# Handing on staging buffers after a modelled delay, two reduction units moved, and rotary's half swap by copies, in a hybrid encoder block

## The chip, the cores and the metric

The kernel runs on one core of one Trainium2 chip. The metric is the device time of one execution in microseconds (us). TensorE (PE) multiplies matrices, VectorE (DVE) and ScalarE (ACT) work on elements, GpSimd (POOL) issues accumulating DMAs here, and SyncE (SP) issues nearly all other DMAs.

## The reference, cut to what matters

The block puts 16 learned tokens ahead of 1024 frames (width 1024) and computes, in float32:

```python
h = h + token_mixer(rmsnorm(h, norm_mix_g), ...)      # 4 mLSTM heads + 4 retention heads
h = h + channel_mixer(rmsnorm(h, norm_ffn_g), ...)    # conv-gated MLP
return rmsnorm(h, norm_final_g)[:, N_META:]

# token_mixer: proj = up @ w_in, split into q, k, v, output gate of each head
# mLSTM heads:     qk = silu(causal_dwconv(q and k)); gated chunk scan; head_norm; * sigmoid(o)
# retention heads: rotary(q), rotary(k); decaying chunk scan; head_norm; * silu(g)
def rotary(t, pos):
    t1, t2 = t[..., : d // 2], t[..., d // 2:]
    return concatenate([t1 * cos - t2 * sin, t1 * sin + t2 * cos], axis=-1)
# then mixed @ w_out;  channel_mixer: (silu(causal_dwconv(u @ w_up)) * (u @ w_gate)) @ w_down
```

## The kernel before

**Matmuls.** Each float32 product is made of three reduced-precision ones (lines L675, L676, L677): every operand is split into a high part (`hi_...`, a cast on ACT, L295) and a rest (`lo_...`, a subtraction on DVE, L300). The big products use Strassen-like sums of 512-wide quarters, so weights are also added and subtracted before use (DVE, L373 to L378).

**Heads.** They are worked on in the order 4, 0, 1, 2, 3, 5, 6, 7 (numbers 0 to 3 are mLSTM heads, 4 to 7 retention heads). For each, PE makes q and k (`pq<h>`), for a pair of heads v (`pv<p>`), and the output gate (`po<h>`). From PE's projections ACT and DVE make `qT` and `kT`: four-tap convolutions (L901, L906) and SiLU (L916) for mLSTM heads, rotary (L915 to L932) for retention heads. Then each head's scan runs over 9 chunks: scores `s` (L1260), `kw` on ACT and `pt` on DVE from them, state update `u`, output `n` (L1309, L1311). At three points of a scan (after chunks 3, 6 and 8) the norm is finished on DVE (L1350) and applied on ACT (L1355), the result is transposed on PE (`tr_0`, `tr_1`, `tr_2`, L1364), multiplied into `mx` on DVE (L1372) and stored to DRAM (`mxd`, L1384).

**Who sets the order.** The Python program deals the work out while it records it. PE's work is the main line (`go`); everything else (`side`: rotary, convolutions, gates, scans) is dealt in between by a planner that compares modelled loads of PE, DVE and ACT (`load`, in us). Generators give up control with `yield` and are moved on once for each PE group (`tick`). `drain` empties the side list at once, with the flag `rush` set. Each engine then runs its list in order, and each DMA queue too: an SP row that waits holds back all SP rows behind it.

**Staging buffers.** Four buffers of 128x1024 take raw weights from DRAM in a fixed list of jobs (`job`, `jload`, L223): a job's load is issued when `jfree` has handed on a buffer. Beside the weights of heads (`raw_q2a` and so on), three kinds of reduction units use these buffers: `w_unit` (L429) loads two blocks of `w_out`, adds them on DVE (L437 to L441) and stores four sums (`wsw`, L443); `m_unit` (L401) loads two blocks, scales and adds them for the meta tokens (L414 to L418) and accumulates them into DRAM (`accd`, a DMA of POOL, L424); `first_right` (L469) loads finished mixer rows (`raw_fr`) and stores their parts (`rone`, `diff`). In the kernel before, `jfree` directly follows the stores, so the next load of a buffer stands right behind them on SP and waits there until they have landed.

**After the heads** comes the product with `w_out` (`pwx`, `pwy`; weights `raw_w_0`, `raw_w_2`, L1072, split as `hi_w` on ACT, L575) and then the MLP (`pup`, `pga`, `pd`), from about 750 us to the end.

Of the kernel before, what the change touches and what calls it, by code (L numbers as in the profile page):

```python
# [65 lines left out]
def body(ctx, tc, h_in, vecs, cst, mask_in, rot, w_v0, w_vp, w_g, w_out, w_up, w_gate, w_down, out):  # L66
# [17 lines left out]
    last = {}  # L84
# [130 lines left out]
    def jload():  # L215
        while jfreed and len(jraw) < min(len(jobs), jcap[0]):
            i = len(jraw)
            nm, srcs = jobs[i]
            jslot[i] = jfreed.pop(0)
# [51 lines left out]
    def busy():  # L271
        return not rush[0] and max(load["DVE"], load["Activation"]) - load["PE"] > 0.5

# [127 lines left out]
    def m_unit(h):  # L401
# [3 lines left out]
        def make():  # L405
            assert {k, k + 1} <= posted, k

            def g():
                yield from jwait(*js)
                x0, x1 = (jget(j) for j in js)  # L410
                for j in range(2):
# [7 lines left out]
                    yield  # L419
                for i, x in enumerate((x1, x0)):  # L420
                    if h == 4:
                        nc.sync.dma_start(accd[i], x)
                    else:
                        G.dma_start(accd[i], x, accum_op=ALU.add)  # L424
                jfree(*js)
# [3 lines left out]
    def w_unit(k):  # L429
        js = [job(f"w{k + 8 * i}", w_out[k + 8 * i]) for i in range(2)]  # L430

        def make():
            def g():
# [7 lines left out]
                V.tensor_tensor(v12, v12, v11, ALU.add)  # L441
                for x, st_, o in ((v22, "65", HB), (v21, "73", HB), (v11, "65", 0), (v12, "73", 0)):
                    nc.sync.dma_start(sums["w", st_, k][:, o:o + HB], x)  # L443
                jfree(*js)
# [24 lines left out]
    def first_right(k):  # L469
        i = job(f"fr{k}", mxd[k])  # L470

        def make():
            assert k in posted, k
            hi, lo = half_tiles(f"fr{k}")

            def g():
# [5 lines left out]
                V.tensor_tensor(a[:, HB:], a[:, :HB], a[:, HB:], ALU.subtract)  # L482
                nc.sync.dma_start(rone[k][:, :HB], hi.bitcast(F32))
                nc.sync.dma_start(rone[k][:, HB:], lo.bitcast(F32))
                nc.sync.dma_start(diff[k], a[:, HB:])
                jfree(i)
# [49 lines left out]
    for f in w_units(3):  # L536
        f()
    u_fm("o", 4, *v_units(0, 0))
    prev = 4
    for p, (a, b) in enumerate(PAIRS):  # L540
# [4 lines left out]
        u_fm("o", b, *(v_units(p + 1, 0) if p < 2 else r_units(2, 3)), *m_units(a))  # L545
# [93 lines left out]
    def first_norm(r):  # L639
# [13 lines left out]
        for i, x in enumerate(xs):  # L653
# [3 lines left out]
            last.setdefault("first", m)  # L657
# [123 lines left out]
    def sig_tasks(h):  # L781
        def f(b):
            AC.activation(sigt[:, b], sigt[:, b], AF.Sigmoid if h < H else AF.Silu)
            done.add(("sig", h, b))
# [104 lines left out]
    def qk_tasks(h):  # L889
# [29 lines left out]
        def rotary(i, r):  # L919
# [5 lines left out]
            V.tensor_tensor(t[0:64, a:b], x[64:128, a:b], A2[64:128, a:b], ALU.mult)  # L925
# [3 lines left out]
            V.tensor_tensor(d[:, a:b], d[:, a:b], t[:, a:b], ALU.add)  # L929
# [400 lines left out]
    def post_steps(h, p):  # L1330
# [28 lines left out]
        def half(b):  # L1359
# [23 lines left out]
            e = min(t1, MB + HB)  # L1383
            nc.sync.dma_start(mxd[i][:, a0 - MA:e - MA], mx[:, :e - a0])  # L1384
# [836 lines left out]
```

## Time and profile before

| | |
|---|---|
| median of 3 runs | 1546.06 us (1544.81 to 1550.42) |
| the profiled execution's own time | 1552.62 us |
| its span, first to last instruction | 1550.5 us |
| PE busy | 1494.9 us (96%) |
| DVE busy | 1109.5 us (72%) |
| ACT busy | 761.8 us (49%) |
| mean granted TensorE clock | 0.983 |

The profile is of one execution. "Busy" is the time in which an engine executes; a wait is put down to the instruction that released it. `L12` is line 12 of the kernel before; names stand as output<-inputs. `PEq`, `SPq` are the issuing sides of an engine.

### The profile page before, as it was taken

Reading aid. Unit: us, or ns where it says so; the run is one execution under the profiler, and the core shown is the slowest. Engines: PE = TensorE matmul, PEld = TensorE weight load, DVE = VectorE, ACT = ScalarE, POOL = GpSimd, SP = SyncE. Lnnn points to the kernel's source line nnn. Section 1 sums busy time; section 2 is a strip of 40 time slices with the busy share of each in tenths; the row PEclk is TensorE's granted clock in tenths of the full one; section 3 lists DMA queues with packets and bytes.
Section 4 is the critical chain, followed back from the end, with each engine's and each line's share of the span. In section 5 each row is a group of like instructions: output and inputs, shape, how many; then the busy total and the mean of one; then the engine's idle time right before and its main releaser. Section 6 shows DMA issues by size and latency. Waiting matters only on the chain.

```text
span 1550.5 us, 25359 instructions
## 1 busy us (share of the span) xinstructions
PE 1494.9 (96%) x9819; PEld 1357.0 (88%) x9819; DVE 1109.5 (72%) x2156; ACT 761.8 (49%) x1459; POOL 85.1 (5%) x144
## 2 busy tenths in 40 slices
PE   6979999998999989989999999999999999999997
PEld 5979999997999988987888998999999999888887
DVE  8886778765877667755787688766666666778656
ACT  5445666745663545454354455444444444434443
POOL 1000000000000000000000001222220000000000
PEclk9989999999999999999999999999999999999998
DMA  7331265325542356498532327887773223933213
GB/s 264 128 110 56 69 203 160 92 77 169 183 112 83 100 190 187 143 306 319 171 125 100 103 85 227 207 215 197 185 190 88 82 82 131 383 104 115 95 42 109
DMA packets 107176, 232.17 MB, mean 150 GB/s; under 512 B 10808, under 2 KB 34048, under 8 KB 106880
## 3 DMA queue, kind: packets, MB, share of 16 engines
q1 hardware_dynamic: 96736, 201.12, 38.9%
q0 software_dynamic: 10176, 29.37, 9.8%
q8 instruction: 77, 1.26, 0.3%
q14 instruction: 43, 0.35, 0.1%
q10 hardware_dynamic: 144, 0.07, 0.0%
HBM read 179.10 MB, written 74.49 MB: 164 GB/s over the span
## 4 chain that ended last, share of the span: by engine, by line
PE 81%; DMA 9%; DVE 7%; ACT 1%; issue 1%; SPq 0%; DVEq 0%; ACTq 0%
PE pdx L675 3%; PE pdx L677 3%; PE pdx L676 3%; PE pup_x L676 2%; PE pup_x L677 2%; PE pup_x L675 2%; PE pga_x L676 2%; PE pga_x L677 2%; PE pga_x L675 2%; PE pdy L675 2%; PE pdy L677 2%; PE pdy L676 2%; PE pwx L676 2%; PE pwx L675 2%; PE pwx L677 2%; DMA accd<-raw_m 2%
## 5 line engine op out<-in xcount | busy, mean ns | idle before, releaser
L575 ACT CAST hi_up<-raw_up 128x512 fp32r<-128x512 f32 (+1 forms) x52 | 36.4, 719 | 107.2 <-PE pga_z L676 60.3
L576 DVE TENSOR_TENSOR lo_ga<-fraw_ga,hi_ga 128x512 fp32r<-128x512 f32 (+1 forms) x52 | 41.9, 808 | 37.7 <-ACT hi_ga L575 37.5
L675 PE MATMUL pup_x<-uh_g,hi_up 128*128 128x256 f32 (+1 forms) x240 | 67.5, 284 | 1.2 <-ACT uh_g L1625 1.2
L676 PE MATMUL pup_x<-ul_g,hi_up 128*128 128x256 f32 (+1 forms) x240 | 67.5, 283 | 0.1
L576 DVE TENSOR_TENSOR lo_up<-raw_up,hi_up 128x512 fp32r<-128x512 f32 (+1 forms) x52 | 41.2, 809 | 35.9 <-ACT hi_up L575 35.1
L677 PE MATMUL pup_x<-uh_g,lo_up 128*128 128x256 f32 (+1 forms) x240 | 66.6, 283 | 0.0
L576 DVE TENSOR_TENSOR lo_d<-rd,hi_d 128x1024 fp32r<-128x1024 f32 (+1 forms) x34 | 37.7, 1113 | 32.9 <-ACT hi_d L575 32.7
L575 ACT CAST hi_ga<-fraw_ga 128x512 fp32r<-128x512 f32 (+1 forms) x52 | 36.4, 718 | 45.8 <-PE pup_z L676 22.9
L677 PE MATMUL pdx<-uh_d,lo_d 128*128 128x512 f32 (+1 forms) x156 | 57.9, 374 | 0.0
L676 PE MATMUL pdx<-ul_d,hi_d 128*128 128x512 f32 (+1 forms) x156 | 57.6, 373 | 0.0
L575 ACT CAST hi_d<-rd 128x1024 fp32r<-128x1024 f32 (+1 forms) x34 | 32.4, 962 | 49.4 <-PE pdy L676 32.6
L677 PE MATMUL pdy<-uh_d,lo_d 128*128 128x512 f32 x132 | 51.7, 392 | 0.0
L676 PE MATMUL pdy<-ul_d,hi_d 128*128 128x512 f32 x132 | 51.3, 389 | 0.0
L675 PE MATMUL pdx<-uh_d,hi_d 128*128 128x512 f32 (+1 forms) x156 | 49.0, 375 | 0.0
L675 PE MATMUL pdy<-uh_d,hi_d 128*128 128x512 f32 x132 | 48.5, 393 | 0.0
L675 PEld LDWEIGHTS pup_x<-uh_g,hi_up 128*128 128x128 f32 x240 | 45.8, 191 | 2.3 <-ACT uh_g L1625 1.4
L676 PE MATMUL pga_x<-ul_g,hi_ga 128*128 128x512 f32 x120 | 47.6, 397 | 0.0
L677 PE MATMUL pga_x<-uh_g,lo_ga 128*128 128x512 f32 x120 | 47.3, 394 | 0.0
L675 PE MATMUL pga_x<-uh_g,hi_ga 128*128 128x512 f32 x120 | 47.3, 394 | 0.0
L676 PEld LDWEIGHTS pup_x<-ul_g,hi_up 128*128 128x128 f32 x240 | 45.8, 191 | 1.1 <-DVE ul_g L1626 0.3
L677 PEld LDWEIGHTS pup_x<-uh_g,lo_up 128*128 128x128 f32 x240 | 44.9, 190 | 0.8
L1260 PE MATMUL s<-qT,kT 128*128 128x128 f32 (+1 forms) x144 | 27.9, 275 | 11.7 <-DVE kT L929 8.7
(1685 smaller groups left out, 5814.9 us busy)
## 6 DMA issues: line engine op xcount, KB each, us to landing
raw_up<-w_up_d SPq DMA_DIRECT2D x22, 512.0 KB, 4.1
fraw_ga<-w_gate_d SPq DMA_DIRECT2D x22, 512.0 KB, 4.3
acts<-cv SPq DMA_DIRECT2D x44, 256.0 KB, 3.4
wsd<-w_down_d POOLq DMA_DIRECT2D x44, 256.0 KB, 6.4
rd<-wsd SPq DMA_DIRECT2D x22, 512.0 KB, 3.4
raw_w<-w_out_d SPq DMA_DIRECT2D x20, 512.0 KB, 5.8
wsw<-raw_w SPq DMA_DIRECT2D x32, 256.0 KB, 2.0
raw_m<-w_out_d SPq DMA_DIRECT2D x14, 512.0 KB, 3.9
```

Of the source, the lines that this page charges most:

```text
L575: AC.copy(hi[:, o:o + n], x)
L576: V.tensor_tensor(lo[:, o:o + n], x, hi[:, o:o + n].bitcast(F32), ALU.subtract)
L675: m.append(PE.matmul(pt, ah, xh_, start=first and k == 0, stop=False, skip_group_check=True))
L676: PE.matmul(pt, ah, xl_, start=False, stop=False, skip_group_check=True)
L677: m.append(PE.matmul(pt, al, xh_, start=False, stop=last and k == n - 1, skip_group_check=True))
L1260: PE.matmul(s[:, :L], k, q, start=True, stop=True)
```

## The change

1. A generator `lag(us)` is added. It gives up control until the planner's modelled PE load has grown by so many us; outside the planned part and under `rush` it returns at once. It stands ahead of the stores of `w_unit`, `first_right`, of the `mx` rows and ahead of the sigmoids and table loads, and, with 8, 5 and 3 us, between a unit's stores and the `jfree` of its buffers.
2. `m_unit` and the `raw_fr` loads wait in the planner for the rows they need, in place of an assertion.
3. Of three `w_unit`s ahead of all heads, one stays; two move behind the output gates of heads 1 and 3.
4. Rotary's two half-width DVE products become two half-width ACT copies (which swap the halves) and one full-width DVE product; the host table has its signs exchanged.
5. For head 4, the gate tasks are dealt between the first and the second half of rotary, and the planner starts with 4 us on DVE and 2 us on ACT.
6. The eight residual loads are written later in the program (`t == 4`). In the first norm, the mark `last["first"]`, behind which the first weight casts are placed, is set at a later copy.

```diff
+    def lag(us):
+        t = load["PE"]
+        while dealt[0] and not rush[0] and load["PE"] - t < us:
+            yield
...
     def jload():
         while jfreed and len(jraw) < min(len(jobs), jcap[0]):
             i = len(jraw)
             nm, srcs = jobs[i]
+            if nm[:2] == "fr" and int(nm[2:]) not in posted:
+                break
...
     def m_unit(h):
...
-            assert {k, k + 1} <= posted, k
-
             def g():
+                while not {k, k + 1} <= posted:
+                    yield
                 yield from jwait(*js)
...
+                yield
                 for i, x in enumerate((x1, x0)):
                     if h == 4:
                         nc.sync.dma_start(accd[i], x)
                     else:
                         G.dma_start(accd[i], x, accum_op=ALU.add)
+                yield from lag(8)
                 jfree(*js)
...
     def w_unit(k):
...
+                yield from lag(1.5)
                 for x, st_, o in ((v22, "65", HB), (v21, "73", HB), (v11, "65", 0), (v12, "73", 0)):
                     nc.sync.dma_start(sums["w", st_, k][:, o:o + HB], x)
+                yield from lag(5)
                 jfree(*js)
...
     def first_right(k):
...
+                yield from lag(1.5)
                 nc.sync.dma_start(rone[k][:, :HB], hi.bitcast(F32))
                 nc.sync.dma_start(rone[k][:, HB:], lo.bitcast(F32))
                 nc.sync.dma_start(diff[k], a[:, HB:])
+                yield from lag(3)
                 jfree(i)
...
-    for f in w_units(3):
+    for f in w_units(1):
         f()
...
-        u_fm("o", b, *(v_units(p + 1, 0) if p < 2 else r_units(2, 3)), *m_units(a))
+        u_fm("o", b, *(v_units(p + 1, 0) if p < 2 else r_units(2, 3)), *m_units(a), *w_units(p < 2))
...
-            last.setdefault("first", m)
+            if r == 0:
+                last["first"] = m
...
     def sig_tasks(h):
         def f(b):
+            yield from lag(1.5)
             AC.activation(sigt[:, b], sigt[:, b], AF.Sigmoid if h < H else AF.Silu)
...
-            V.tensor_tensor(t[0:64, a:b], x[64:128, a:b], A2[64:128, a:b], ALU.mult)
-            V.tensor_tensor(t[64:128, a:b], x[0:64, a:b], A2[0:64, a:b], ALU.mult)
+            AC.copy(t[0:64, a:b], x[64:128, a:b])
+            AC.copy(t[64:128, a:b], x[0:64, a:b])
             yield
             V.tensor_tensor(d[:, a:b], x[:, a:b], A1[:, a:b], ALU.mult)
+            V.tensor_tensor(t[:, a:b], t[:, a:b], A2[:, a:b], ALU.mult)
             V.tensor_tensor(d[:, a:b], d[:, a:b], t[:, a:b], ALU.add)
...
             mix_into(mx[:, :w], a0, t1)
             e = min(t1, MB + HB)
+            if e < t1:
+                V.tensor_copy(mm[:, i], mx[:, e - a0:w])
+            yield from lag(1.5)
             nc.sync.dma_start(mxd[i][:, a0 - MA:e - MA], mx[:, :e - a0])
...
-    side += qk_tasks(4) + gate_tasks + scan[:12]
+    side += qk_tasks(4)[:2] + gate_tasks + qk_tasks(4)[2:] + scan[:12]
...
-        return [(lambda: tables_load(h), 0, lambda: "gates" in done)]
+        def f():
+            yield from lag(3)
+            tables_load(h)
+        return [(f, 0, lambda: "gates" in done)]
     reset()
+    load.update({"DVE": 4.0, "Activation": 2.0})
     go(o_steps(4))
...
-        if t == 1:
+        if t == 4:
             for kb in range(0, KB, 2):
                 for a, b, o in ((0, SB, 0), (SB, T, 16)):
                     nc.sync.dma_start(RT[kb // 2][:, :, a:b], h_in[:, kb:kb + 2, a + o:b + o])
```

How the planner then deals the work is read from the order of each engine's instructions in the two built programs. Lines of the changed kernel stand some 2 to 18 higher (L690 there is L677 before, L1275 is L1260, L1379 is L1364, L920 is L906, L453 is L443, L225 is L223).

**The start of head 4's scan, on PE.** Before, the first score matmul `s_0` stands right behind the first group of head 0's projection `pq0x`:

```order
L675 MATMUL pq0x_1324<-u11h,hi_o_6_0_996 128x264
L676 MATMUL pq0x_1324<-u11l,hi_o_6_0_996 128x264
L677 MATMUL pq0x_1324<-u11h,lo_o_6_0_997 128x264
L1260 MATMUL s_0_1036<-qT_935,kT_936 128x16
L1265 MATMUL s_0_1036<-cs,kT_936 128x128
L675 MATMUL pq0x_1298<-uS2h,hi_q_1_0_1143 128x264
```

Of the change, on PE, `s_0` stands inside the second group of v (`pv0y`), behind all of head 0's q and k:

```order
L690 MATMUL pv0y_1705<-hi_vp_1_0_1551,u12l 128x256
L688 MATMUL pv0y_1705<-hi_vp_1_0_1551,u12h 128x256
L689 MATMUL pv0y_1705<-lo_vp_1_0_1552,u12h 128x256
L1275 MATMUL s_0_1126<-qT_925,kT_926 128x16
L1280 MATMUL s_0_1126<-cs,kT_926 128x128
L690 MATMUL pv0y_1705<-hi_vp_1_0_1551,u12l 128x256
```

It is the PE's row 481 before and row 659 of the change, so 178 rows later.

**The end of head 4's scan.** Before, on DVE, the norm factor `mv_1` (L1350), for which the transposes `tr_1` wait, stands ahead of the last chunk's `pt_8`:

```order
L1349 RECIPROCAL z_1_1534<-z_1_1534 128x3
L1350 TENSOR_SCALAR mv_1_1361<-mv_1_1361,z_1_1534 128x3
L1320 TENSOR_SCALAR C_7_1537<-C_6_1487,u_7_1529 128x256
L1284 TENSOR_SCALAR pt_8_1511<-s_8_1509,cs 128x128
L906 TENSOR_SCALAR kT_1904<-rawk,vec,kT_1904 128x527
L906 TENSOR_SCALAR kT_1904<-rawk,vec,kT_1904 128x512
```

Of the change, on DVE, `pt_8` stands eleven rows ahead of `mv_1` (L1365 there); between them are the splits and sums of head 0's gate weights (three rows ahead of these: `lo_o` twice and one L920, as well) and the convolution taps of head 0's `kT`:

```order
L381 TENSOR_TENSOR raw_o0a<-raw_o0a,raw_o0b 128x512
L920 TENSOR_SCALAR kT_1884<-rawk,vec,kT_1884 128x512
L1364 RECIPROCAL z_1_1540<-z_1_1540 128x3
L1341 BN_STATS bn_7_1546<-v4hi 128x6
L920 TENSOR_SCALAR kT_1884<-rawk,vec,kT_1884 128x526
L384 TENSOR_TENSOR raw_o0a<-raw_o0a 128x512
L920 TENSOR_SCALAR kT_1884<-rawk,vec,kT_1884 128x512
L1341 BN_STATS bn_8_1574<-v4hi 128x6
L1365 TENSOR_SCALAR mv_1_1372<-mv_1_1372,z_1_1540 128x3
```

Behind `mv_1` DVE has two small rows, four L920, one small row and two more L920, and only then `mx_1_0` (L1387 there). Before, on PE, some fifty matmuls of `pv0y` and `pv0x` stand among `s_8`, `n_8`, `tr_1_0` and `tr_1_1`. Of the change, on PE, nothing stands among them:

```order
L1275 MATMUL s_8_1517<-qT_925,kT_926 128x128
L1324 MATMUL n_7_1537<-v4hi,pt_7_1473 128x256
L1326 MATMUL n_7_1537<-C_6_1499,qT_925 128x256
L1324 MATMUL n_8_1567<-v4hi,pt_8_1519 128x256
L1326 MATMUL n_8_1567<-C_7_1543,qT_925 128x256
L1379 MATMUL tr_1_0_1641<-cs,v4lo 128x128
L1379 MATMUL tr_1_0_1641<-cs,v4hi 128x128 x2
L1379 MATMUL tr_1_1_1666<-cs,v4lo 128x128
L1379 MATMUL tr_1_1_1666<-cs,v4hi 128x128 x2
L688 MATMUL pv0y_1705<-hi_vp_5_0_1908,uS4h 128x256
```

What moved is the PE work: the scan now ends at a `drain`, where none is left to stand beside it.

**The loads of head 2's q and k, on SP.** `raw_q2a` is the first weight block of `pq2x`. Before:

```order
L223 DMA raw_m_2965<-w_out_d 128x1024
L1384 DMA mxd_88<-mx_2_1_2772 128x254
L223 DMA raw_m_3009<-w_out_d 128x1024
L223 DMA raw_q2a<-w_g_d 128x1024
L223 DMA raw_q2b<-w_g_d 128x512 x2
L223 DMA raw_vp_11_3127<-w_vp_d 128x1024
```

Of the change, on SP, a moved `w_unit` stands ahead of it, and the buffer that `raw_q2a` takes is that of its second and third stores:

```order
L225 DMA raw_m_2936<-w_out_d 128x1024
L225 DMA raw_m_2969<-w_out_d 128x1024
L225 DMA raw_w_2975<-w_out_d 128x1024
L225 DMA raw_w_3014<-w_out_d 128x1024
L453 DMA wsw_3_151<-raw_w_3014 128x512
L453 DMA wsw_3_159<-raw_w_2975 128x512
L453 DMA wsw_3_151<-raw_w_2975 128x512
L453 DMA wsw_3_159<-raw_w_3014 128x512
L225 DMA raw_q2a<-w_g_d 128x1024
L225 DMA raw_vp_11_3205<-w_vp_d 128x1024
L225 DMA raw_vp_21_3207<-w_vp_d 128x1024
L225 DMA raw_q2b<-w_g_d 128x512 x2
```

Two loads and four stores came ahead of `raw_q2a`; `raw_q2b` now stands behind two loads that take the buffers of the accumulates. `raw_q5a` shows the same change.

More of the change, by code (lines that the diff above doesn't have):

```diff
@@ L472, in make @@
         def make():
-            assert k in posted, k
             hi, lo = half_tiles(f"fr{k}")
@@ L1383, in half @@
             e = min(t1, MB + HB)
+            if e < t1:
+                V.tensor_copy(mm[:, i], mx[:, e - a0:w])
+            yield from lag(1.5)
             nc.sync.dma_start(mxd[i][:, a0 - MA:e - MA], mx[:, :e - a0])
             if e < t1:
-                V.tensor_copy(mm[:, i], mx[:, e - a0:w])
                 posted.add(i)
@@ L2172, in _lay @@
     c, s = np.cos(ang), np.sin(ang)
-    a["rot"] = np.stack([np.concatenate([c, c], 0), np.concatenate([s, -s], 0)], 1).astype(np.float32)
+    a["rot"] = np.stack([np.concatenate([c, c], 0), np.concatenate([-s, s], 0)], 1).astype(np.float32)
     w = f("w_in")[0].reshape(2, 4, P, -1)
```

## The prediction

> **What bounds the kernel now.** I read the page's busy times first, then the table of stretches, then PE's waits, longest first.
>
> ```profile
> PE 1494.9 (96%) x9819; PEld 1357.0 (88%) x9819; DVE 1109.5 (72%) x2156; ACT 761.8 (49%) x1459; POOL 85.1 (5%) x144
> ```
>
> PE is busy for 96% of the span, so the change can win or lose time only where PE stands idle or runs at a lower clock. Columns below: stretch, length, busy time of PE, PEld, DVE, ACT, POOL, granted clock, DMA share, GB/s.
>
> ```profile
> 50.00:75.00 25.00, 25.00 (x212) 25.00 (x211) 24.16 (x36) 9.85 (x16) 0.00 (x0) 1.00 0.26 86
> 98.00:120.00 22.00, 13.27 (x85) 12.00 (x84) 18.26 (x38) 8.22 (x17) 0.00 (x0) 0.77 0.15 48
> 225.00:245.00 20.00, 18.81 (x146) 17.63 (x145) 16.32 (x37) 16.83 (x34) 0.29 (x2) 1.00 0.62 202
> 375.00:400.00 25.00, 19.55 (x136) 18.02 (x135) 16.20 (x41) 15.58 (x32) 1.25 (x3) 0.93 0.84 261
> 530.00:565.00 35.00, 31.04 (x213) 29.46 (x212) 21.97 (x50) 18.53 (x35) 1.72 (x2) 0.90 0.57 172
> 600.00:660.00 60.00, 55.90 (x410) 52.83 (x410) 43.32 (x101) 27.06 (x62) 0.86 (x1) 1.00 0.54 159
> 680.00:700.00 20.00, 16.29 (x98) 15.01 (x96) 7.01 (x22) 10.92 (x23) 0.00 (x0) 0.83 1.04 366
> 950.00:1540.00 590.00, 589.99 (x3446) 521.03 (x3445) 409.94 (x643) 261.56 (x460) 54.05 (x77) 1.00 0.52 151
> ```
>
> From 950 us on PE has no idle time at all: the MLP is out of the question. The idle time lies in the heads: 8.7 us in the second row, 5.5 in the fourth, 4.0 in the fifth, 4.1 in the sixth, 3.7 in the seventh. PE's waits name the releasers (total, times, longest):
>
> ```profile
> PE s L1260 <- DVE kT L929: 8.7, 1, 8.7
> PE pq3x L675 <- ACT hi_o L295: 4.0, 1, 4.0
> PE n L1309 <- ACT n L1322: 3.7, 1, 3.7
> PE pq6x L675 <- ACT hi_o L295: 2.7, 1, 2.7
> PE pq6x L677 <- DVE lo_o L300: 1.2, 1, 1.2
> ```
>
> A stall costs more than its idle time, because the clock falls behind it:
>
> ```profile
> 104.80:115.00 10.20, 4.33 (x20) 4.33 (x21) 8.95 (x19) 1.42 (x4) 0.00 (x0) 0.50 0.32 104
> 388.10:391.50 3.40, 3.30 (x15) 3.30 (x16) 2.54 (x7) 3.34 (x6) 0.00 (x0) 0.50 0.66 251
> 551.90:558.80 6.90, 5.97 (x27) 5.98 (x28) 5.23 (x12) 6.04 (x11) 0.00 (x0) 0.51 0.20 74
> 688.50:695.30 6.80, 5.15 (x20) 4.78 (x21) 3.48 (x9) 5.67 (x9) 0.00 (x0) 0.50 1.04 387
> ```
>
> PE busy at half clock loses half of that time. So head 4's first score costs 8.7 + 2.2 = 10.9 us, head 3's q (`pq3x`) 4.0 + 1.65 = 5.65, head 6's q 2.7 + 1.2 + 3.0 = 6.9, and `n` 3.7 + 2.6 = 6.3.
>
> **The change part by part.** Sums are made against the profiled execution, 1552.6 us (span 1550.5); the median of the runs shown is 6.6 lower, and I carry the difference over to it. Half a per cent, about what a measurement can tell from no change, is 7.7 us.
>
> *Head 4's first score.* DVE has no gap before it: it is the DVE queue that is late with `kT`.
>
> ```profile
> L925 DVE TENSOR_TENSOR kT<-rawq,A x8: 686/695/704, 98.0 to 640.7; 64x528 f32<-64x528 f32 x4, 64x512 f32<-64x512 f32 x4
> ...
> L374 DVE TENSOR_TENSOR raw_o0a<-raw_o0a,raw_o0b 128x512 f32<-128x512 f32 x1 | 0.7, 680 | 0.0
> ...
> L295 ACT CAST hi_vp<-raw_vp 128x512 fp32r<-128x512 f32 x12 | 6.8, 620 | 3.3 <-PE pv0y L677 1.4 <-PE pq0x L676 1.0 <-ACT gsm L1002 0.9
> ```
>
> Two half-width products of 0.695 become one of full width, which I take at the same price: 0.7 less in each of 4 places, 2.8 us of DVE per head. The two units moved away take eight sums of L374's shape (0.68, so 5.4) off DVE as well. And `s_0` stands 178 PE rows later, some 20 us at the 25.00/212 = 0.12 us of the 50 to 75 stretch. 8.2 + 20 us is far over 8.7, so the stall goes: **-10.9** (bounds -10.9 and -8). The 32 ACT copies are not in the trace; the nearest row is the cast of 0.62, so 20 us on an ACT that is half idle, at nothing; at DVE's 0.7 they take 22. Where ACT is late, at most one pair (1.4) is added to a head.
>
> *The end of head 4's scan.* The order shows no PE work between `s_8` and `tr_1_1` but six matmuls and transposes, and on DVE between `pt_8` and `mv_1` two `lo_o`, four taps, L374, L377 and two statistics; then six taps and `mx_1_0`.
>
> ```profile
> L300 DVE TENSOR_TENSOR lo_o<-raw_o0a,hi_o 128x512 fp32r<-128x512 f32 x5 | 3.3, 685 | 0.7 <-ACT hi_o L295 0.7
> L906 DVE SCALAR_TENSOR_TENSOR kT<-rawk,vec,kT 128x512 f32<-128x512 f32 x6 | 4.5, 745 | 0.1
> L1326 DVE BATCH_NORM_STATS2 bn<-v4hi 128x6 f32<-128x256 f32 x4 | 1.7, 424 | 0.7 <-ACT v4hi L1322 0.7
> L1372 DVE SCALAR_TENSOR_TENSOR mx<-tr,vec,sig 128x384 f32<-128x384 f32 x4 | 2.4, 612 | 0.0
> L1355 ACT ACTIVATE v4hi<-v4hi,mv,z 128x256 f32<-128x256 f32 x4 | 2.2, 590 | 0.0
> ```
>
> To `mv_1`: 2 x 0.685 + 2 x 0.68 + 4 x 0.745 + 2 x 0.424 = 6.6, and 0.6 for L1355; PE has about 1.4 of its own work there: 5.8 idle. From `mv_1` to `mx_1_0`, for which `tr_1_1` waits: 6 x 0.745 + 0.6 and small rows, 5.5, less 0.7 of transposes: 4.8. Behind it `pv0y` waits for ACT, which has two table loads and four passes in that time, about 0.7 more. With the 2.2 of clock that followed the 8.7 us stall: **+13.5** (bounds +8, if half of the taps have run earlier, and +17). These rows follow from the order of one queue, so I hold this term for the surest.
>
> *The loads behind moved units.* `raw_q2a` and `raw_q5a` now wait for a unit's third store.
>
> ```profile
> wsw<-raw_w SPq DMA_DIRECT2D x32, 256.0 KB, 2.0
> ...
> wsw<-raw_w SPq DMA_DIRECT2D x4, 256.0 KB, 6.5
> accd<-raw_m POOLq DMA_DIRECT2D x2, 512.0 KB, 8.1
> ...
> raw_q6a<-w_g_d SPq DMA_DIRECT2D x1, 512.0 KB, 5.0
> ```
>
> The first row is the page's, the others are those of 533 to 551 us, where a unit's stores met the accumulates of `accd`: 6.5 in place of 2.0. Such a store and the load behind it take 11.5 us; this is how head 3's and head 6's q came to stall before. In the change heads 2 and 5 have the same rows in the same order (stores, accumulates between them, load). I price each at head 3's 5.65: **+11.3** for both (bounds 0, if the store takes 2.0, and 2 x 6.9). Queued behind `raw_q2a` on SP stand `raw_vp_11`, `raw_vp_21`, which wait for accumulates, and `raw_q2b`, which is used some 6 us of PE work later: covered. The Trainium skill, page "DMA: Bandwidth & Descriptors", section "Queues, rings and completion order", says that each DMA engine serves its queue rows in turn, packet by packet: a store beside one accumulate would then take about 4, an estimate from the 2.0, and both terms together fall to some 6. The row of 6.5 speaks against it.
>
> *Head 1's q.* Its cast now stands on ACT behind head 0's last norm, a table load, a sigmoid and two passes of L1355, and later behind the eight L883.
>
> ```profile
> L783 ACT ACTIVATE sig<-sig 128x1026 f32<-128x1026 f32 x2 | 2.1, 1056 | 0.0
> L916 ACT ACT_TABLE_LOAD x3 | 3.8, 1283 | 1.1 <-DVE qT L906 1.1
> L883 ACT ACTIVATE A<-A,cols 128x128 f32<-128x128 f32 x16 | 5.0, 392 | 3.2 <-DVE A L877 3.2
> ```
>
> 1.28 + 1.06 + 1.2 + 0.6 = 4.1 and a norm of about 2 ahead, beside 2 us of PE work: 4 idle; 1 more for the second load and the L883. With head 3's clock loss, and less the 1.2 us that 225 to 245 shows idle now: **+5.5** (bounds 0 and +9).
>
> *Head 6's q.* The accumulates now stand behind all four stores, and `raw_fr` behind the load: of 6.9 I take **-4.5** (bounds -6.9 and 0).
>
> *`n` at 686.* What is late is not ACT itself:
>
> ```profile
> 688.78 1.04 ACT L575 CAST hi_w<-raw_w 128x1024 fp32r<-128x1024 f32 x1 [7.49 <-DMA raw_w<-w_out_d]
> L1072 SPq DMA_DIRECT2D raw_w<-w_out_d x1: 383/383/383, 673.9 to 673.9; - x1
> ```
>
> ACT waited 7.5 us in its queue for `raw_w_2`, issued at 673.9 behind eight `wone` loads, and the copy of `n` stood behind. In the change that load directly follows `raw_w_0` and the cast stands behind two more copies of `n`: **-6.3** (bounds -6.3 and 0). Next late is that cast's product, `pwx`, not before the scan's end.
>
> *The rest.* 600 to 660 us holds head 7's rotary, and 4.1 idle; 2.8 less on DVE give back **-2** (bounds -4 and +1.4). Head 3's own rows stay as they were. The later sigmoids, table loads and `mx` stores are waited for by no PE row above; the residual loads move by a few rows on SP; the first norm's mark by one cast: nothing, 2 us either way.
>
> Sum: -10.9 + 13.5 + 11.3 + 5.5 - 4.5 - 6.3 - 2 = +6.6, so 1559.2 in a profile like this one and **1553** as a median.
>
> **The rivals.** *The loads land in time* (faster). If the third store leaves before the accumulates fill the engines, it takes 2.0; `raw_q2a` and `raw_q5a` then come ahead of need, and head 1 loses 1.5. This decides below some 2.6 us of store time. -11.3 - 4: the sum is -8.7, **1537**. For it: the page's median of 2.0; against it: the 6.5. *Half shares*, by the queue rule above: a store of 4.0 leaves about 1.5 idle per head, so the sum falls by 2 x 2.5 to +1.6, **1548**. *The late loads are worse* (slower): heads 2 and 5 at head 6's 6.9 (+2.5), head 1 at 9 (+3.5) and `n` still held by a `raw_w` (+6.3), since 680 to 700 shows the DMA engines at 1.04: +19, **1565**. It decides if the casts of head 1's q find `raw_q1b` not landed. *The change does not do what it says*: excluded for the handing on, since the order shows loads behind the delays; but in a `drain` the delay is nothing.
>
> **How the numbers follow.** Forecast 0.45 (own range 1546 to 1560), in time 0.20, half shares 0.08, worse 0.27. Half of the forecast's chance lies above 1553.8. Faster by over 0.5%: most of "in time" and little else, 0.17. Slower: 0.22 of the forecast and 0.26 of the worse case, 0.48. Within: 0.35. The range reaches from "in time" to a little over "worse": 1537 to 1567.
>
> **What would show it.** The list of PE's waits after: `s` on `kT` gone; `tr` on `z` or `mv` (about 6) and on `mx` (about 4) near 160 us; `pq2x`, `pq5x` on `hi_o` at about 4; `pq1x` on ACT; `n` on ACT gone. I am wrong if the scan's end shows below 6 us, or if `pq2x` and `pq5x` do not wait.

## The result, and the profile after

The changed kernel takes 1560.88 us (median of 7 runs, 1553.46 to 1567.7), the kernel before 1548.18 us in 7 runs of the same sessions: a ratio of 1.0085, 95% interval 1.0057 to 1.0113. It is slower by 0.85%. The profiled execution took 1560.88 us (span 1559.1, mean granted clock 0.981), so 8.3 us more than the profiled execution before. One of the 12 executions of experiment 2 below took 2086.91 us, at a granted clock of 0.654; its ratio leaves it out.

The page's busy times after:

```profile
PE 1496.5 (96%) x9819; PEld 1360.9 (87%) x9819; DVE 1099.6 (71%) x2140; ACT 778.2 (50%) x1488; POOL 84.1 (5%) x144
```

DVE has 10 us less to do and ACT 16 more; the 32 copies alone take 20.0 us on ACT (0.626 each), as forecast. PE is again busy 96% of the time; busy times do not show where 8 us went. The table of stretches does (same columns as in the prediction; L675 of before is L688 here, L1364 is L1379, L1372 is L1387):

```profile
98.00:120.00 22.00, 22.00 (x179) 21.43 (x179) 18.58 (x48) 12.26 (x23) 0.10 (x1) 1.00 0.15 49
150.00:190.00 40.00, 31.59 (x197) 27.43 (x196) 26.97 (x67) 22.12 (x43) 0.43 (x3) 0.83 0.13 41
215.00:250.00 35.00, 29.98 (x208) 28.53 (x207) 21.64 (x55) 21.09 (x42) 0.47 (x3) 0.85 0.69 224
250.00:290.00 40.00, 37.18 (x288) 34.74 (x287) 29.71 (x64) 20.11 (x41) 2.50 (x6) 0.96 0.62 186
440.00:470.00 30.00, 27.23 (x199) 25.18 (x198) 21.03 (x52) 14.05 (x29) 2.55 (x6) 1.00 0.57 159
565.00:600.00 35.00, 28.42 (x217) 27.67 (x216) 21.27 (x39) 15.63 (x29) 0.00 (x0) 0.90 0.66 214
600.00:660.00 60.00, 57.77 (x434) 54.93 (x433) 47.79 (x112) 39.56 (x85) 1.72 (x2) 1.00 0.55 163
680.00:700.00 20.00, 20.00 (x150) 18.58 (x149) 11.70 (x28) 9.94 (x25) 1.72 (x2) 1.00 0.89 267
```

The first and the last row are the two places that were to be cured: 8.7 and 3.7 us of idle time are gone, at full clock. The five rows from 150 to 600 us are the price: 8.4 us idle at the end of head 4's scan, then 5.0, 2.8, 2.8 and 6.6 ahead of the q of heads 1, 2, 5 and 6. The list of PE's waits (total, times, longest) names them:

```profile
PE pq6x L688 <- DVE sig L758: 6.0, 1, 6.0
PE pq3x L688 <- ACT hi_o L302: 4.6, 1, 4.6
PE pq1x L688 <- ACT hi_o L302: 3.9, 1, 3.9
PE tr L1379 <- ACT v4lo L1370: 3.8, 1, 3.8
PE tr L1379 <- DVE mx L1387: 3.2, 2, 2.6
PE pq2x L688 <- ACT hi_o L302: 2.8, 1, 2.8
PE pq5x L688 <- ACT hi_o L302: 2.8, 1, 2.8
```

`s` on `kT` and the long `n` on ACT have left the list. The rows in their place are those that the prediction named, but for `pq3x`, which waited before too, and `pq6x`, which was to get better.

What each place is worth is read, as in the prediction, from the time that PE loses there: its idle time, and half of its busy time at a granted clock of 0.5. PE's work without these losses is nearly the same in both profiles (1476.6 and 1476.2 us), so the losses hold the whole difference but for 0.4 us. Both profiles are read over the same stretches; the changed kernel comes to the same work up to 20 us later, and the edges lie where PE loses nothing in either.

| place | predicted, us | lost before | lost after | change |
|---|---|---|---|---|
| head 4's first score (98 to 120 us) | -10.9 | 10.9 | 0.0 | -10.9 |
| end of head 4's scan (150 to 190) | +13.5 | 0.0 | 12.1 | +12.1 |
| head 1's q (215 to 250) | +5.5 | 1.2 | 8.8 | +7.6 |
| head 2's q (250 to 290) | +5.65 | 0.0 | 4.4 | +4.4 |
| head 5's q (440 to 470) | +5.65 | 0.0 | 2.8 | +2.8 |
| head 6's q (530 to 600) | -4.5 | 7.0 | 8.4 | +1.4 |
| head 7's rotary (600 to 680) | -2 | 4.8 | 2.2 | -2.6 |
| `n` at 686 us (680 to 700) | -6.3 | 6.3 | 0.0 | -6.3 |
| 830 to 850 us | 0 | 0.0 | 3.4 | +3.4 |
| all else (parts of about 3 us at most, of both signs) | 0 | 43.7 | 40.8 | -2.9 |
| **sum** | **+6.6** | **74.0** | **82.9** | **+9.0** |

### The profile page after: what moved, and what is told of

The parts are those of the page before. It is cut to its first block, busy times and chain, and to the rows that moved or that the text cites. A ratio compares the mean times of both kernels' runs of the same rounds, so it can differ in the third digit from the quotient of the medians.

```text
span 1559.1 us, 25372 instructions
## 1 busy us (share of the span) xinstructions
PE 1496.5 (96%) x9819; PEld 1360.9 (87%) x9819; DVE 1099.6 (71%) x2140; ACT 778.2 (50%) x1488; POOL 84.1 (5%) x144
## 4 chain that ended last, share of the span: by engine, by line
PE 79%; DMA 12%; DVE 7%; ACT 1%; issue 1%; SPq 0%; DVEq 0%; POOL 0%; ACTq 0%
PE pdx L688 3%; PE pdx L690 3%; PE pdx L689 3%; PE pup_x L689 2%; PE pup_x L690 2%; PE pga_x L689 2%; PE pup_x L688 2%; PE pga_x L688 2%; PE pga_x L690 2%; PE pdy L688 2%; PE pdy L690 2%; PE pdy L689 2%; PE pv L726 2%; PE pwy L689 1%; PE pwy L690 1%; DMA accd<-raw_m 1%
## 5 line engine op out<-in xcount | busy, mean ns | idle before, releaser
L688 PE MATMUL pup_x<-uh_g,hi_up 128*128 128x256 f32 (+1 forms) x240 | 67.1, 282 | 1.2 <-ACT uh_g L1646 1.2
L690 PE MATMUL pup_x<-uh_g,lo_up 128*128 128x256 f32 (+1 forms) x240 | 66.4, 283 | 0.0
L690 PE MATMUL pdx<-uh_d,lo_d 128*128 128x512 f32 (+1 forms) x156 | 58.0, 375 | 0.0
L690 PE MATMUL pdy<-uh_d,lo_d 128*128 128x512 f32 x132 | 51.8, 392 | 0.0
L688 PE MATMUL pdx<-uh_d,hi_d 128*128 128x512 f32 (+1 forms) x156 | 49.0, 376 | 0.0
L688 PE MATMUL pdy<-uh_d,hi_d 128*128 128x512 f32 x132 | 48.6, 394 | 0.0
L688 PEld LDWEIGHTS pup_x<-uh_g,hi_up 128*128 128x128 f32 x240 | 45.4, 189 | 2.2 <-ACT uh_g L1646 1.4
L690 PE MATMUL pga_x<-uh_g,lo_ga 128*128 128x512 f32 x120 | 47.3, 395 | 0.0
L688 PE MATMUL pga_x<-uh_g,hi_ga 128*128 128x512 f32 x120 | 47.3, 395 | 0.0
L690 PEld LDWEIGHTS pup_x<-uh_g,lo_up 128*128 128x128 f32 x240 | 44.6, 188 | 0.8
L690 PEld LDWEIGHTS pdx<-uh_d,lo_d 128*128 128x128 f32 x156 | 29.3, 188 | 5.6
```

What stands on the lines that cost most here:

```text
L688: m.append(PE.matmul(pt, ah, xh_, start=first and k == 0, stop=False, skip_group_check=True))
L690: m.append(PE.matmul(pt, al, xh_, start=False, stop=last and k == n - 1, skip_group_check=True))
```

## The experiments

Theory A says that the order costs the time: the units that were moved stand ahead of the loads of q, and the side work of head 4 piles up on DVE at the end of its scan. Theory B says that the delays do: everything that is queued later comes later. Times are medians, ratios are to the kernel before, run on the same chip. What one version wins on another goes by their ratios, since the kernel before itself had medians from 1545.33 to 1548.18 us.

**1. No delays.**

```diff
-        while dealt[0] and not rush[0] and load["PE"] - t < us:
-            yield
+        yield from ()
```

> The changed kernel with all its delays at nothing (lag returns at once), all else kept. Theory A, the order: the stall at the end of head 4's scan comes from the DVE queue that the units, the rotary and the gates leave there, and the waits of pq2x and pq5x from the w units that now stand ahead of their loads. Neither needs a delay: near 160 us tr waits about 4 and 2.6 us again (13 us lost there in all), pq2x and pq5x wait about 3 us each, and the time is that of the changed kernel within 4 us. Theory B, the delays: stores, table loads and buffers that come later are what costs; without them the stall at the scan's end and the two waits are gone, and the time falls by 8 us or more, to that of before. Head 6's q: by A its load is as late as in the changed kernel (6 us of wait); by B it waits 3 us or less.

1566.33 us, ratio 1.0123 (1.0100 to 1.0145): the slowest of all, 0.4% above the changed kernel, though the two intervals just overlap (that one ends at 1.0113). Of its waits of PE:

```profile
PE pq5x L687 <- ACT hi_o L301: 4.5, 1, 4.5
PE tr L1378 <- ACT v4lo L1369: 3.8, 1, 3.8
PE n L1323 <- ACT n L1336: 3.3, 1, 3.3
PE pq2x L687 <- ACT hi_o L301: 0.9, 1, 0.9
```

The stall at the scan's end is there to the tenth (3.8), so Theory B falls for it. But A missed half of the rest: without delays `pq2x` waits 0.9 and `pq6x` is not in the list, `pq5x` waits more, and `n` is back. The delays move the waits of q from head to head: at head 6 Theory B had it right (below), at heads 2 and 5 and at `n` neither had. On the whole the delays seem to help; they are not the main cost.

**2. Without the planner's lead at head 4.**

```diff
-    load.update({"DVE": 4.0, "Activation": 2.0})
```

> The changed kernel without the one line that starts the planner of head 4's steps with 4.0 us of DVE and 2.0 us of ACT work on its account, so that it spreads the side work earlier. Theory A, the order: with it the DVE queue at the scan's end is short, since the two weight halves and taps stand elsewhere: near 160 us the tr rows wait no more than 1 us and only n (about 1.2) and pv0y (about 2) wait; 9 us are won there, head 1's q wins 1 to 4 more, pq2x and pq5x wait as in the changed kernel (about 3 us each). The time falls by 8 to 12 us, to about that of before. Rival, the rotary's copies or the moved units alone hold the scan's end: nothing changes there, the time stays within 3 us of the changed kernel.

1551.82 us, ratio 1.0020 (1.0006 to 1.0033): 10 us won with one line. The same stretch as above, in this kernel's table:

```profile
150.00:190.00 40.00, 37.78 (x282) 34.84 (x282) 27.23 (x62) 23.65 (x45) 0.39 (x3) 1.00 0.16 54
```

2.2 us idle in place of 8.4, at full clock: PE loses 2.2 at the scan's end in place of 12.1. So, with all else as changed, the line that accounts 4 us to DVE before head 4 lets the sums, the taps and the splits pile up where PE has nothing else to do. Around head 1's q 7.5 us are lost (190 to 250 us) in place of 8.8, the low end of the 1 to 4 that were to be won; PE there no longer waits for the load, but for DVE (`s` on `pt` 2.1, `tr` on `mx` 1.6).

**3. The old rotary in the changed kernel.**

```diff
-            AC.copy(t[0:64, a:b], x[64:128, a:b])
-            AC.copy(t[64:128, a:b], x[0:64, a:b])
+            V.tensor_tensor(t[0:64, a:b], x[64:128, a:b], A2[64:128, a:b], ALU.mult)
+            V.tensor_tensor(t[64:128, a:b], x[0:64, a:b], A2[0:64, a:b], ALU.mult)
             yield
             V.tensor_tensor(d[:, a:b], x[:, a:b], A1[:, a:b], ALU.mult)
-            V.tensor_tensor(t[:, a:b], t[:, a:b], A2[:, a:b], ALU.mult)
...
-    a["rot"] = ... np.concatenate([-s, s], 0) ...
+    a["rot"] = ... np.concatenate([s, -s], 0) ...
```

> The changed kernel with the rotary of before (two half-width products on DVE, no copies on ACT, the table's sign as before), all else kept. DVE has 2.8 us more per head, ACT 32 copies less. Theory A, the order at one place counts: head 4's first scores wait about 3 us (pq0x), the scan's end loses about 3 in place of 13 because the planner deals the weight halves differently, head 1's q loses 3 to 6: the time falls by 4 to 8 us. Rival, the rotary only moves 22 us from DVE to ACT, and PE waits at the same places: the scan's end still loses 13 and the time is within 3 us of the changed kernel, or above it by up to the 2.8 us of DVE at head 7.

1553.18 us, ratio 1.0037 (1.0018 to 1.0055): 7 us less, with DVE 2.8 us more loaded in each of four heads. The scan's end loses 1.8 (12.1 in the changed kernel), 5.1 are lost around head 4's first scores, from 85 to 120 us (none), and 7.3 at head 1's q (8.8), where 3 to 6 were expected. As A had it, what counts is not the 2.8 us of DVE: the rotary changes what the planner deals where, and so what stands at the scan's end.

**4. The two moved units back at the start.**

```diff
-    for f in w_units(1):
+    for f in w_units(3):
...
-*m_units(a), *w_units(p < 2))
+*m_units(a))
```

> The changed kernel with its two moved w units back ahead of the heads (three at the start, none beside heads 2 and 5), all else kept. Theory A: pq2x and pq5x no longer wait (7 us won with their clock), the scan's end loses about 5 (pv0y on ACT) in place of 13 and head 1's q 2 in place of 7; but the 5.4 us of DVE work return ahead of head 4's first score, where about 7 us are lost (3 at the gate transposes, 4 at pq0x) and 2 of clock: in all 8 to 12 us less than the changed kernel. Rival, the loads are late by the accumulates alone, whatever stands ahead of them: pq2x and pq5x still wait 2 us or more each, and the gain is 5 us or less.

1550.02 us, ratio 1.0009 (0.9991 to 1.0026): 12 us won, and no longer to be told from the kernel before. Its list of PE's waits has no row of `pq2x` or `pq5x`, and in their place:

```profile
PE pv0y L688 <- ACT v L756: 4.3, 1, 4.3
PE n L1324 <- ACT n L1337: 3.8, 1, 3.8
PE pq0x L688 <- ACT rawq L754: 3.4, 1, 3.4
```

**5. The moved units alone, in the kernel before.**

```diff
-    for f in w_units(3):
+    for f in w_units(1):
...
-*m_units(a))
+*m_units(a), *w_units(p < 2))
```

> The kernel before with one part of the change alone: the two w units moved behind the output gates of heads 1 and 3, no delay, the old rotary, the old place of the gates. Theory A, each place has its own price: 5.4 us of DVE work less ahead of head 4's first score, whose wait falls from 8.7 to 2 to 3 us (with the clock, 8 us won); the scan's end loses 3 to 4 (pv0y on ACT), pq2x and pq5x wait 3 to 4 us each with 1 us of clock (8 lost), n near 690 us still waits. In all 1 to 6 us above the kernel before. Rival, the moved units are the part that helps and all else costs: 5 us or more below the kernel before.

1557.21 us, ratio 1.0080 (1.0052 to 1.0108): as slow as the whole change. The size was a miss, 10.5 us between the medians where 1 to 6 were expected; the places were not:

```profile
PE pq5x L675 <- ACT hi_o L295: 3.9, 1, 3.9
PE pq2x L675 <- ACT hi_o L295: 3.4, 1, 3.4
PE n L1309 <- ACT n L1322: 3.0, 1, 3.0
PE pv0y L675 <- ACT v L743: 2.4, 1, 2.4
```

PE loses 3.6 us from 85 to 120 us in place of 10.9, since `kT` is waited for 0.7 us in place of 8.7; it loses 2.4 at the scan's end, 5.1 at head 2's q and 5.6 at head 5's, where it lost nothing before. These places do not add up to 10.5: this profile (span 1551.7) is of one of the fast executions of its kernel, that of before (1550.5) of one of the slowest.

Runs 4 and 5 say the same from both sides: the moved units cost about 0.8%, and all the rest of the change together about 0.1%, within what can be measured of nothing. But the prices of the parts do not add: of the 13 us of the whole change, taking out the units alone gives back 12 (run 4), the planner's lead alone 10 (run 2), the new rotary alone 7 (run 3). The parts act through one order of the work, so each price holds only beside the others.

**6. The w unit ahead of the m unit.** What makes the load behind a moved unit late? Here the units stay where the change put them, but the one with the plain stores comes first:

```diff
-*m_units(a), *w_units(p < 2))
+*w_units(p < 2), *m_units(a))
```

> The changed kernel with each moved w unit written ahead of the m unit beside it, not behind it, so that its two loads and four stores come before the two accumulates; raw_q2a and raw_q5a still stand directly behind the fourth store on SP, and raw_q2b and raw_q5b no longer behind the vp loads. Theory A, the loads of heads 2 and 5 are late because the unit's last stores and then the load itself run beside the accumulates: stores land in about 2 us each, the load is issued earlier and takes about 5, pq2x and pq5x wait under 1 us each: 6 to 7 us less than the changed kernel (perhaps 2 given back at head 2's first transposes, where two taps more stand on DVE). The scan's end near 160 us and head 1's q stay as they were. Rival, it is the unit itself, its buffers and its four DVE sums ahead of the load: pq2x and pq5x wait 2 us or more as before and the time is within 3 us of the changed kernel.

1552.75 us, ratio 1.0045 (1.0029 to 1.0061): 6 us won. Its list of PE's waits has no `pq2x` and no `pq5x`, while `pq1x` (3.0), `tr` (3.8 and 2.6) and `pq6x` (5.2) stay. In the transfers of the changed kernel ahead of head 5's q, issued from 446 to 450 us (KB, median us from issue to landing)

```profile
accd<-raw_m POOLq DMA_DIRECT2D x2, 512.0 KB, 7.4
wsw<-raw_w SPq DMA_DIRECT2D x2, 256.0 KB, 4.8
raw_q5a<-w_g_d SPq DMA_DIRECT2D x1, 512.0 KB, 8.2
```

the load runs beside both accumulates and takes 8.2 us. In run 6 it leaves SP before them (window 437.5 to 443 us):

```profile
accd<-raw_m POOLq DMA_DIRECT2D x2, 512.0 KB, 9.0
raw_q5a<-w_g_d SPq DMA_DIRECT2D x1, 512.0 KB, 3.9
wsw<-raw_w SPq DMA_DIRECT2D x1, 256.0 KB, 2.0
```

Half the time, while the accumulates take 9.0 in place of 7.4, for which PE does not wait. But the load also leaves earlier against the time at which it is needed. From four traces, in us (lead: from the load's issue to the time at which PE was ready for the first matmul of q):

| | head 2: lead | load took | head 5: lead | load took |
|---|---|---|---|---|
| kernel before | 19.1 | 6.5 | 20.7 | 8.0 |
| changed kernel | 5.1 | 7.2 | 6.1 | 8.2 |
| run 5 | 5.9 | 8.6 | 5.1 | 8.3 |
| run 6 | 9.9 | 3.7 | 9.6 | 3.9 |

In the kernel before these loads took nearly as long as in the changed one, and PE did not wait for them: what they lost by the moved unit, as run 5 shows too, is 13 to 16 us of lead. From landing to matmul takes 0.7 us (cast and split). So, as an estimate from these rows, either half of run 6's gain would have been enough: 9.6 us of lead for a load of 8.2, or a load of 3.9 with 6.1 us of lead. Run 6 does not tell them apart; both come from writing the w unit first.

**7. and 8. Other places for the units**, both without the planner's lead of run 2. In run 7 they stand behind q of heads 2 and 5 (`u_fm("q", a, *w_units(p > 0))`), in run 8 beside the units behind q of heads 1 and 3 (`w_units(2)` there).

> The changed kernel without the planner's 4.0 and 2.0 us at the start (as in the run without the queue's lead), and with the two moved w units one stage later: behind the loads of q of heads 2 and 5, in front of those of v, and no longer in front of q's. Theory A: both costs of the order go. Near 160 us only n and pv0y wait (2 to 3 us in all, 10 less than the changed kernel), pq2x and pq5x wait under 1 us (7 less); head 3's and head 6's q stay as they are. 16 us less than the changed kernel: 1543 to 1547, at or just under the time of before. Rival, the units' loads and stores cost the same wherever they are put, since the DMA engines are what is full: the v stage of heads 2 and 5 (pv1x, pv2x) then waits 3 us or more each, and only the 10 us of the scan's end are won, 1550.

> As the run before it in this list, but the two moved w units stand beside the ones that are already behind q of heads 1 and 3 (two there in a row, in front of the output gate's loads). Theory A: pq2x and pq5x wait under 1 us, the scan's end 2 to 3, and the output gates of heads 1 and 3 have the slack for a load that comes 8 us later: 1543 to 1548. Rival, the output gate's loads are now the late ones: po1x and po3x wait 3 us or more each, 1550 or more.

1547.57 us, ratio 1.0014 (0.9994 to 1.0033), and 1549.64 us, ratio 1.0020 (1.0000 to 1.0040). 11 and 10 us less than the changed kernel and no `pq2x` or `pq5x` in either list, nor the `pv1x`, `pv2x`, `po1x` and `po3x` of the two rivals; but both stay above the times that Theory A named (1543 to 1547, and 1543 to 1548). Part of the gain came back as waits of `s` on `pt` (6.7 us in 4 places in run 7).

**9. All of it together.** Run 7, and the remaining units behind the output gates of heads 0, 2 and 5 turned round as in run 6.

```diff
-*v_units(p, 1), *m_units(prev), *w_units(1))
+*v_units(p, 1), *w_units(1), *m_units(prev))
```

> The run with the units behind q of heads 2 and 5 and without the planner's lead, and in addition the remaining w units beside the m units (behind the output gates of heads 0, 2 and 5) written ahead of them. Theory A, the waits of pq3x (4.0 us, 8 with the clock) and pq6x (4.7 us, 7.5 with the clock), which the kernel before has too, have the cause that the w unit ahead of the m unit took away at heads 2 and 5: under 1 us each is left, 3 to 5 us of short waits for ACT stay at head 3's q, and 2 to 4 appear at head 1's output gate, where ACT is late with the copies of pq1x. 5 to 9 us less than that run: a ratio to the kernel before of 0.993 to 0.999, faster than both kernels. Rival, at heads 3 and 6 the load is late for another cause (the rows of raw_fr, or buffers): pq3x and pq6x still wait 3 us or more and the ratio is 1.000 to 1.003.

1555.02 us, ratio 1.0061 (1.0040 to 1.0081): a clear miss, 7 us slower than run 7. The wait of `pq3x` on its load fell to 0.3 us, as expected; that of `pq6x` did not, and other rows came:

```profile
PE s L1275 <- DVE pt L1294: 6.6, 3, 3.6
PE n L1324 <- ACT n L1337: 4.6, 1, 4.6
PE pq6x L688 <- DVE sig L758: 4.2, 2, 2.3
```

ACT waits 4.6 us for `raw_q6a` there. `n` at 686 us is back. ACT's row for the first weight cast of that stretch, in run 9:

```profile
688.16 1.04 ACT L587 CAST hi_w<-raw_w 128x1024 fp32r<-128x1024 f32 x1 [7.64 <-DMA raw_w<-w_out_d]
```

and in the changed kernel:

```profile
693.51 1.05 ACT L587 CAST hi_w<-raw_w 128x1024 fp32r<-128x1024 f32 x1 [2.57 <-DMA raw_w<-w_out_d]
```

In all ten profiles with the changed kernel's order of these casts, `n` waits as long as this cast less 3.0 us: 4.6 for 7.6 here, 2.0 for 5.0 in run 2, 0.4 for 3.4 in the second profile of the changed kernel (run 11), and nothing where the cast waits less than 3.0 (the first profile of the changed kernel, runs 3 and 7). So the cure of `n` hangs on a margin of 0.4 us in one load. What decides that load was not settled.

**10. The same line in the kernel before.** The diff of run 9, and nothing else.

> The kernel before with one line changed: the w units beside the m units behind the output gates of heads 0, 2 and 5 written ahead of them. Nothing else. Theory A: pq3x waits under 1.5 us in place of 4.0, pq6x under 1 in place of 3.9, and with their clock 6 to 10 us are won; head 1's q may lose 2 to 4 by ACT. The ratio to the kernel before is 0.994 to 0.999. Rival: the loads wait as they did, ratio 1.000 or more.

1546.29 us, ratio 1.0007 (0.9997 to 1.0017): no gain either, although both load waits are gone. Of PE's waits:

```profile
PE tr L1364 <- DVE mx L1372: 7.6, 8, 2.6
PE pq6x L675 <- ACT rawq L741: 2.5, 1, 2.5
```

`pq3x` (4.0 before) is not in the list, and `pq6x` now waits for ACT. `tr` on `mx`, 0.8 us before, has grown to 7.6 in 8 places: the load is there in time and PE waits for DVE a little later. At these places a wait was moved rather than removed. None of the versions is faster than the kernel before; runs 4, 7 and 10 cannot be told from it.

**11. and 12. Second profiles**, of the changed kernel and of the kernel of run 5, both unaltered.

> The changed kernel unaltered, for a second profile: its runs lie 14 us apart. If only the clock differs from one execution to the next, the waits of PE come at the same rows with the same lengths within 1 us (tr 3.8 and 2.6, pq6x 6.0, pq3x 4.6, pq1x 3.9, pq2x and pq5x 2.8) and the difference lies in stretches with a granted clock below 1: above all the 32 one-column matmuls near 840 us, which took 4.86 us there and 3.62 in the kernel before. If the transfers differ, the waits of pq2x, pq5x, pq3x and pq6x change by 1 us or more.

> The kernel before with the two moved units alone, unaltered, for a second profile: the profiled execution of it lay 2 us above the kernel before, the median of its runs 10. If the clock makes the difference, the waits of pq2x (3.4), pq5x (3.9), pq3x (5.2), pq6x (3.9) and n (3.0) stay as they are and stretches at a granted clock of about 0.5 appear elsewhere; if the transfers do, these waits are 2 us or more longer in all.

1555.94 us (span 1554.2) where the first profile of the changed kernel had 1560.88, and 1556.96 us (span 1555.1) where that of run 5 had 1553.51. In the changed kernel the waits come at the same rows:

```profile
PE pq6x L688 <- DVE sig L758: 5.4, 1, 5.4
PE pq2x L688 <- ACT hi_o L302: 2.7, 1, 2.7
```

None of those in the first list differs by more than 0.6, and the stretch 150 to 190 us reads 31.59 busy at 0.83 in both. The 4.9 us between the two spans are not the clock: PE is idle for 62.6 us in the first and 58.0 in the second, in small parts of which the opening, to 60 us, is the largest (13.7 against 12.4), while half clock costs 20.3 and 20.8, in part at other places (3.4 and 1.7 us from 830 to 850 us, nothing and 1.7 from 440 to 470). Over the 7 timed runs the span does go with the mean granted clock (1551.7 us at 0.984; 1555.6, 1558.2 and 1559.1 at 0.981; 1560.2, 1562.9 and 1565.9 at 0.977); which of the two causes the other these runs do not show. In run 12 `pq2x` waits 1.3 more than in run 5, the others 0.4 less or 0.2 more; its span is 3.4 longer, 1.9 of it by the clock.

## Why the prediction came out as it did

The direction and most of the places were right. The conversion into a median was not, head 6 went the other way, and the waits at heads 1, 2, 5 and 6 had in part other causes. The forecast was 1553.0, the runs gave 1560.88: inside the whole range, 0.9 above the forecast's own (1546 to 1560).

**The sum and the median.** The sum gave 1559.2 for a profiled execution, and the profiled execution took 1560.88. The step that failed is the sentence that carries over the 6.6 us between the profile and the median. It took the profile of before, one of the slowest executions of that kernel, as if a profile always were 6.6 above the runs; the profile after was the median itself. That is 6.2 of the 7.9 us of error. A second profile shows how loose it is: 1560.88 and 1555.94 of one kernel. From median to median the change costs 12.7 us, nearly twice the 6.6.

That the sum came so close to the first profile is in part luck. Its eight places came to +8.5, but by errors that cancel: heads 2 and 5 together 4.1 too high and the scan's end 1.4, head 6 5.9 too low and head 1 2.1. The waits that were named as signs came, and smaller: `tr` 3.8 and 2.6 for 6 and 4, `pq2x` and `pq5x` 2.8 each for 4.

**Head 4's first score** (-10.9, measured -10.9) and **the end of its scan** (+13.5, measured +12.1) went by the rows that were worked out. DVE's rows after, start, duration, operation:

```profile
163.52 1.28 DVE L307 TENSOR_TENSOR lo_o<-raw_o0a,hi_o 128x512 fp32r<-128x512 f32 x2
164.72 0.76 DVE L920 SCALAR_TENSOR_TENSOR kT<-rawk,vec,kT 128x527 f32<-128x527 f32 x1
165.40 0.69 DVE L381 TENSOR_TENSOR raw_o0a<-raw_o0a,raw_o0b 128x512 f32<-128x512 f32 x1
...
168.33 0.75 DVE L920 SCALAR_TENSOR_TENSOR kT<-rawk,vec,kT 128x512 f32<-128x512 f32 x1
...
169.33 0.15 DVE L1365 SCALAR_TENSOR_TENSOR mv<-mv,z 128x3 f32<-128x3 f32 x1
```

These are the two splits, four taps and two sums of the working, back to back; the first transpose starts at 170.2. The idle time was 1.4 + 3.8 + 2.6 + 0.6 against 5.8 + 4.8 + 0.7, so the count was 2.9 long; the clock took 3.7 where 2.2 were counted. Without the planner's lead these rows do not pile up here (run 2), but neither do they with the old rotary (run 3): taking away either is enough to move them.

**Heads 2 and 5** (+5.65 each, measured +4.4 and +2.8): the step that failed is the price of the third store, taken as 6.5 from one row. At head 2 the stores issued from 274.5 to 279.5 us show

```profile
wsw<-raw_w SPq DMA_DIRECT2D x2, 256.0 KB, 3.9
```

and at head 5 the third took 2.0 (the 4.8 under run 6 is the middle of 2.0 and 7.5). The rival "the loads land in time" had put the point of decision at 2.6 us of store time, and head 5 lies under it; yet `raw_q5a` was late, since it met the accumulates itself and took 8.2 us, not the 5.0 of the working. From the third store's issue to the load's landing it took 11.2 and 10.7 us, against 11.5 worked out: too long a store and too short a load made up for each other. The rule of the Trainium skill, page "DMA: Bandwidth & Descriptors", section "Queues, rings and completion order", that each DMA engine serves its queue rows in turn, fits head 2's store, 3.9 beside accumulates against 2.0 alone. It does not give the 7.5 of head 5's fourth store, nor the 6.5 that the working started from.

**Head 6's q** (-4.5, measured +1.4): the same oversight about the load. The step took the accumulates standing behind all four stores as relief for the load behind them. What came is in ACT's rows, each ending in the wait ahead of the cast:

```profile
229.45 0.62 ACT L302 CAST hi_o<-raw_q1a 128x512 fp32r<-128x512 f32 x1 [3.20 <-DMA raw_q1a<-w_g_d]
457.53 0.62 ACT L302 CAST hi_o<-raw_q5a 128x512 fp32r<-128x512 f32 x1 [4.57 <-DMA raw_q5a<-w_g_d]
571.23 0.62 ACT L302 CAST hi_o<-raw_q6a 128x512 fp32r<-128x512 f32 x1 [9.66 <-DMA raw_q6a<-w_g_d]
```

The third store was faster (4.3 in place of 6.5), but the load, issued at 561.7, landed some 9.5 us later beside both accumulates; before it had taken 5.0. Its lead was even longer than before (5.3 against 4.0 us), so here it is the load's own time that costs. PE's list puts this wait down to `sig` on DVE; ACT's row names the load. Run 1, without the delays, issues the load at 559.8, as the accumulates begin, and it lands after 5.2 us: no such wait, but more at `pq5x` and `n`.

**Head 1's q** (+5.5, measured +7.6): somewhat short in size, wrong in cause. The working counted ACT's queue, 4.1 us of table load, sigmoid, norm passes and the cast itself. The first row of the last fence shows ACT done and waiting 3.20 us for `raw_q1a`, which shared the engines with an accumulate and three other transfers issued from 216.5 to 219.5 us:

```profile
raw_w<-w_out_d SPq DMA_DIRECT2D x1, 512.0 KB, 10.7
raw_q1a<-w_g_d SPq DMA_DIRECT2D x1, 512.0 KB, 11.1
wsw<-raw_w SPq DMA_DIRECT2D x1, 256.0 KB, 10.9
A<-scr SPq DMA_DIRECT2D x1, 8.0 KB, 10.3
```

In the kernel before it was issued at 211.3, ahead of that crowd, which began at 212.9, and took 6.0 us. The rival "the late loads are worse" had a late load here, but named `raw_q1b`; its price of 9 was not reached.

**`n` at 686** (-6.3, measured -6.3) and **head 7's rotary** (-2, measured -2.6) came in the size worked out, the first by the margin of 0.4 us named under run 9. That the second is DVE's shorter queue was not tried apart.

**Not in the sum:** 3.4 near 845 us, which is the clock (below), and -2.9 in small parts.

## What to carry to other kernels

Reduction work that is moved off one critical place takes its DMAs along: before it is moved, look at which load is issued behind it, how much lead that load loses and which transfers it will share the engines with, and try to let plain stores and loads leave ahead of accumulates, which won 6 us at two places here (run 6) and nothing at others (runs 9 and 10). Look at what falls due together at the end of a scan when a planner is told to be late. Take a profiled execution's distance to the median as scatter, not as a constant: a forecast of the median starts from the median. And do not add up the prices of parts that were each taken out alone.

## What the runs showed of the hardware

The clock fell where PE had no idle time. The stretch of 32 one-column matmuls in the MLP (`pe<-cs,acc`), in the first profile of the changed kernel and what follows it:

```profile
840.80:845.80 5.00, 5.00 (x34) 4.96 (x34) 1.68 (x4) 0.85 (x2) 0.00 (x0) 0.72 0.00 0
845.80:850.00 4.20, 4.20 (x11) 3.30 (x12) 2.87 (x8) 4.05 (x8) 0.00 (x0) 0.52 0.78 293
```

The same matmuls, and what follows them, in the second profile of the same kernel:

```profile
837.40:841.20 3.80, 3.80 (x35) 3.75 (x34) 1.63 (x4) 0.72 (x2) 0.00 (x0) 1.00 0.00 0
841.20:845.20 4.00, 4.00 (x12) 3.10 (x12) 2.67 (x8) 3.83 (x8) 0.00 (x0) 0.57 0.76 285
```

Here the clock falls just behind them. They took 3.6 us in ten of the fourteen profiles and 4.8 to 4.9 in four, and both in one program. In these four a stretch of 6.8 us at half clock begins during them; in five others one of 3.4 us begins at most 0.8 us behind the last; the remaining five have none near, among them one of the two profiles of run 5's kernel. The profile has PE busy throughout in all fourteen. The Trainium skill, page "TensorE: Matmul & The Clock Gate", section "What's actually happening", ties the drop to an idle window of about 3.4 us; here no idle time goes with it. That a column of one element is little work for the array may be the reason; it was not tried by itself.
